# A hybrid decoder layer on one core: row multiplies behind the weights' low halves, rotary steps beside a head's values

## The chip, the cores and the metric

The kernel runs on one core of one Trainium2 chip. The metric is the time of one execution on the device in microseconds (us), taken as the median of several runs. A profiled execution is one more run, of which every instruction is known. The engines of the core are TensorE (PE, with PEld for the loads of its weights), VectorE (DVE), ScalarE (ACT), GpSimd (POOL) and SyncE (SP, which only starts transfers); GpSimd starts transfers too (POOLq).

## The reference, cut to what matters

The kernel computes one layer for 512 prompt tokens and 8 x 8 new tokens, together 576 columns, in float32: a half-step FFN, a mixer and a second half-step FFN, each behind an RMS norm that is modulated by a conditioning vector.

```python
h = modulate(rms_norm(x, n1_g), sh1, sc1)
x = x + 0.5 * g1 * swiglu(h, w1_gate, w1_up, w1_down)
h = modulate(rms_norm(x, nm_g), sh2, sc2)
mix, S_new, v_rows = token_mix(h, pos0, S0, w_in, ...)
...
def token_mix(h, pos0, S0, w_in, ...):
    z = h @ w_in
    u, v, q, k, rv, rg, ga, gb = jnp.split(z, SPLIT_POINTS, axis=-1)
    ...
    qh = rotary(q.reshape(B, L, RET_HEADS, RET_DK), pos)
    kh = rotary(k.reshape(B, L, RET_HEADS, RET_DK), pos) * (RET_DK ** -0.5)
    vh = rv.reshape(B, L, RET_HEADS, RET_DV)
    o_r, S_new = retention(qh, kh, vh, S0)
    o_b = head_rms(o_r).reshape(B, L, RET_V) * jax.nn.silu(rg)
    merged = jax.nn.sigmoid(ga) * (o_a @ w_a) + jax.nn.sigmoid(gb) * (o_b @ w_b)
    return merged @ w_o, S_new, v
```

Here `rms_norm(x)` is `x` times one norm per token (a row of 576 numbers) times a gain per channel, and `modulate` multiplies and adds one number per channel. Of rotary the lower and the upper 64 channels of a head of 128 are turned into each other by tables of sines and cosines. There are eight heads with 128 channels of q and k and 256 of values each.

## The kernel before

Channels lie on partitions and the 576 tokens along the free dimension; a product runs in two halves of 288 columns (half 0 and half 1). The matmuls take float32 split into a high and a low part (hi, lo), and each product is the sum of three: high by high, low by high and high by low. Weights come as float32 into `wraw` by SyncE's transfers. ScalarE casts the high part (L180, L662, `W.hi`), VectorE subtracts it for the low part (L181 in `split_w`, L668 or L672 in `put_lo`). Activations are split in the same way (L188 and L189, L557 and L564).

The program goes through these stages, in us of the profiled span: the first FFN and the end of it, `last_down1` (to 446); the *streams* (446 to 750), projections of the normed `x` for q and k of all heads, the heads' gates and the merge's gates, each stream two column blocks of 128, with the results stored to memory by GpSimd's queue; the eight heads (750 to 1130), each with its values, its scores, its output and some work of other parts beside it; the rest of the merge (to 1270); `w_o` and the second FFN.

**The end of the first FFN.** `last_down1` gives each step a name, and the string `INTO_MIX` (L51ff.) is the written order of them. `D31` is the product of `w1_down` for block 3, half 1, with 18 matmuls of 288 columns; `rs31` its residual add, `sq31` and `ad31` the square and its sum for the next norm, `sp31` the store of `x` to `x1d`. `Wh4` and `Wl4` are the high and low parts of the weights of block 4. `rd0` is the matmul that sums the squares of half 0 over the channels (L437); `q00` to `q20` make the norm of it, `x00` and so on the normed operand, `N11h0` (L557 and L564 for the second) its split, and `h0a0` the first product of the streams. A loop at L1194 loads the weights' blocks in the order 2, 3, 6, 7, 4, 5.

**The streams.** `stream` takes the pairs one by one, each 144 matmuls of 288 columns, and lets generators work beside it by due times in us. One of them is `operands_of_values` (L1239). The heads' values are products of the whole normed `x`, and this generator makes it from memory, block by block: the row of norms (`row`, from `rowd`) is loaded by GpSimd's queue, and so is block `c` of `x` (`x1d`, L1248). Then VectorE multiplies the block by the row (L1254), ScalarE modulates the prompt's columns (L1256), VectorE the new tokens' (L1260, twice), ScalarE casts the high part (L1262) and VectorE makes the low one (L1264). The multiply of block `c` is written behind the load of block `c + 1`, about a stream apart. In a stream ScalarE also does the copy `sn` (L653) of a partial sum, which a matmul needs next, casts of weights (L662) and the sigmoid or silu at the end (L1155).

**The heads.** For each head, `fetch` loads q and k of the head, as stored by the streams. `rotary` (L1315) is six VectorE instructions for the two: L1317 and L1318 multiply halves by the sines into a new block `y`, L1319 multiplies by the cosines, and GpSimd adds the two (L1320). In the code it stands in the work of the head before, at its end. `values_of` makes the head's values (L1342: four products of 24 matmuls), `core` the scores (L1370, which need k and q), and so on. The output parts are split and multiplied beside this. L1505 is the matmul of the new tokens' state update and L1509 the sum of it with the old state on VectorE; these sums free the banks in which the matmuls accumulate, and L478 is the matmul of products that use the bank after.

**What sets the order.** The code is written as one sequence, and a scheduler lets instructions on VectorE, ScalarE and GpSimd change places when one is free before the other. `in_order` adds an order between two instructions without a wait, and `run` keeps the order of the named steps. Buffers come from pools: `slot` hands out a ring of blocks of 576 columns one after another, and a block is free again when its readers are through.

Of the kernel before, what the change touches and what calls it, by code (L numbers as in the profile page):

```python
# [49 lines left out]
"""  # L50
INTO_MIX = """
D00 D01 rs00 Wh2 sp00 sq00 ad00 Wl2 D10 rs01 px0 Wh3 sq01 ad01 Wl3 D11 sp01 rs10 sp10 sq10
ad10 Wh6 D20 rs11 Wl6 px1 sq11 sp11 ad11 D21 Wh7 rs20 sq20 Wl7 sp20 ad20 D30 rs21 Wh4 px2
sq21 Wl4 sp21 ad21 D31 rs30 sq30 sp30 ad30 Wh5 Wl5 D40 rs31 px3 sq31 sp31 nh0 D50 ad31 rs40
sq40 nl0 sp40 ad40 D60 rs50 sq50 wh0 ad50 sp50 wl0 D70 rs60 sq60 sp60 nh1 ad60 D41 rs70 nl1
sq70 sp70 ad70 D51 rs41 wh1 px4 sq41 wl1 sp41 ad41 rd0 rs51 D61 rq0 px5 q00 sq51 q10 sp51
ad51 q20 x00 D71 x10 b000 b010 x20 b100 x30 b110 N11h0 rs71 N11h1 rs61 px7 b210 N11l0 px6
sq71 N11l1 sq61 sp61 sp71 b300 ad61 h0a0 b310 b200 ad71 B21h3 B21h2 B21l3 B21l2 rd1 sn0 h0a1
rq1 q01 q11 q21 x01 h0b0 x11 b01 b00 s0 b11 s1 b10 tx0 sn1 tx1 N1h0 x21 h0b1 N1h1 N1l0 N1l1
b20 x31 b21 T2a1 b31 b30 h1a0 s3 e0s1 s2 B22h3 N3c1 B22h2 T2b1 N3h1 B22l2 p2bh T2h1 B22l3  # L60
# [21 lines left out]
def layer_kernel(ctx: ExitStack, tc: tile.TileContext, a):  # L82
# [95 lines left out]
    def split_w(raw, eng=None):  # L178
        hi, lo = high_low(list(raw.shape[1:]))
        ACT.copy(out=hi, in_=raw)  # L180
        (eng or DVE).tensor_tensor(out=lo, in0=raw, in1=hi.bitcast(F32), op=ALU.subtract)  # L181
        return hi, lo

    def load_w(src, k0, kc, c0, cols, eng=None):
# [471 lines left out]
    class Weights:  # L656
# [8 lines left out]
        def put_lo(self, names):  # L665
            hl, src, neg = self.hl[names]
            if neg:
                DVE.scalar_tensor_tensor(  # L668
                    out=hl[:, 1], in0=src, scalar=-1.0, in1=hl[:, 0].bitcast(F32), op0=ALU.mult, op1=ALU.subtract
                )  # L670
            else:
                DVE.tensor_tensor(out=hl[:, 1], in0=src, in1=hl[:, 0].bitcast(F32), op=ALU.subtract)  # L672
            for i, m in enumerate(names):
                self.w[m] = (hl[:, 0, i], hl[:, 1, i])

# [510 lines left out]
    def last_down1(W, product):  # L1186
        finish(rest)
        gate, g, ps, rest_of = gate1m(), a2(), {}, {}
        warm(AF.Abs_reciprocal_sqrt)
        ops.clear()  # L1190
        ops["near"] = ("B22", "N3", "N4")
        O = Operands(g, 3)
        steps = {}
        for c in (2, 3, 6, 7, 4, 5):  # L1194
            W.load(c)
            steps[f"Wh{c}"] = lambda c=c: W.hi(c)
            steps[f"Wl{c}"] = lambda c=c: W.lo(c)
        w = rg(0), rg(1)
        p = {i: Plain2(w[i][0], i, w[i][1].out, w[i][1].post) for i in range(2)}
        pairs[3] = p[2] = pair2(qk(0))  # L1200
        steps.update(operand_steps(O))
        ends = pair_steps(p, None)
        for n in ("Gh0", "Gl0", "Gh1", "Gl1"):
            ends.pop(n)
        steps.update(ends)
        for c, h in LAST:
            def d(c=c, h=h):
                ps[c, h] = product(c, h)

            def rs(c=c, h=h):  # L1210
                rest_of[c] = resid(xs[c], ps[c, h], c, h, gate)

            steps[f"D{c}{h}"], steps[f"rs{c}{h}"] = d, rs
            steps[f"sq{c}{h}"] = lambda c=c, h=h: n2.square(xs[c], h)
            steps[f"ad{c}{h}"] = lambda h=h: n2.sum(h)
            steps[f"sp{c}{h}"] = lambda c=c, h=h: nc.scalar.dma_start(out=x1d[:, c, HALF[h]], in_=xs[c][:, HALF[h]])
            if h:
                steps[f"px{c}"] = lambda c=c: rest_of[c]()
        for h in range(2):
            norm_steps(steps, n2, O, h)  # L1220

            def q2(h=h):
                n2.q(2, h)
                POOL.dma_start(out=rowd[:, HALF[h]], in_=n2.r[h])

            steps[f"q2{h}"] = q2
        run(INTO_MIX, steps)
# [11 lines left out]
    def operands_of_values():  # L1239

        g = a2()
        row = slot([P, T])
        POOL.dma_start(out=row, in_=rowd)
        come = []
        for c in range(KC + 1):
# [5 lines left out]
                yield 14.0  # L1251
                continue
            c, t = c - 1, come[c - 1]
            DVE.tensor_tensor(out=t, in0=t, in1=row, op=ALU.mult)  # L1254
            yield 2.0
            ACT.activation(  # L1256
                out=t[:, 0:NP], in_=t[:, 0:NP], func=AF.Identity, scale=g[:, c, 0:1], bias=mT[:, 24 + c, 0:1]
# [55 lines left out]
        return t  # L1313

    def rotary(x):  # L1315
        rope, y = tks["rope"], slot([P, T])
        DVE.tensor_tensor(out=y[0:64], in0=x[64:128], in1=rope[64:128, 1], op=ALU.mult)  # L1317
        DVE.tensor_tensor(out=y[64:128], in0=x[0:64], in1=rope[0:64, 1], op=ALU.mult)  # L1318
        DVE.tensor_tensor(out=x, in0=x, in1=rope[:, 0], op=ALU.mult)  # L1319
        POOL.tensor_tensor(out=x, in0=x, in1=y, op=ALU.add)  # L1320
# [9 lines left out]
            S0.append(t)  # L1330
        tks["states"] = hc, S0

    def values_of(hd, wv):
        rv = []
        for n in range(4):
            ps = bank()
# [7 lines left out]
            if n % 2 == 0:  # L1344
                rv.append(slot([P, 2, DV]))
            ACT.copy(out=rv[n // 2][:, n % 2, :], in_=ps[:, :DV])
            tick(24 * 0.109)
        rvs = rts[0].tile([P, DV], F32, tag="rvs", name=nm("rvs"), bufs=2)
        ps = bank()
# [340 lines left out]
    for hd in range(HEADS):  # L1690
        wv = [load_w(win, 4 * i, 4, RV0 + hd * DV, DV) for i in range(2)]
        if hd:
            states(hd)
        rv, rvs = values_of(hd, wv)
        if hd == 0:
            for x in rows[0][:2]:
                rotary(x)
        OBs.append([])
        q, k, *gates = rows.pop(hd)
        prev = core(hd, q, k, gates, rv, rvs, OBs[hd])  # L1700
# [5 lines left out]
        for i, (weights, f) in enumerate(work):  # L1706
# [7 lines left out]
                    fetch_mixers()  # L1714
            if i == len(work) - 2 and i:
                ready = work[i + 1][0]()
                for x in rows[hd + 1][:2]:
                    rotary(x)
        if len(work) == 2:
            for x in rows[hd + 1][:2]:  # L1720
                rotary(x)
        if hd + 1 < HEADS:
            finish(prev)
        if hd == HEADS - 2:
# [323 lines left out]
```

## Time and profile before

| | us |
|---|---|
| median of 3 runs | 1682.55 |
| lowest and highest | 1680.50, 1685.21 |
| the profiled execution | 1680.16 |
| its span in the trace | 1678.3 |
| TensorE busy (98%) | 1641.8 |
| VectorE busy (69%) | 1156.4 |
| ScalarE busy (47%) | 785.2 |
| GpSimd busy (17%) | 291.0 |

The span is the time from the first to the last instruction of the trace, and the profiled execution's own time holds the 1.9 us around it too. The mean granted clock of TensorE is 0.996 of full speed over the span. The busy time is the sum of the durations of an engine's instructions: the instructions of one engine stand in one queue, so an instruction that waits holds back all behind it. A wait is shown in square brackets behind an instruction, as the idle time of the engine before it and what ended that. The rows are in the section before the prediction.

### The profile page before, as it was taken

What the parts mean: (1) busy time and instruction counts of PE and PEld (TensorE: products, weight loads), DVE (VectorE), ACT (ScalarE), POOL (GpSimd) and SP (SyncE); (2) the same over time, 40 slices, a digit from 0 to 9 for tenths busy, and PEclk for the clock granted to TensorE, in tenths of its full rate; (3) what the DMA queues carried; (4) which work ended last, traced back from release to release, by engine and by line L of the source; (5) the groups of instructions that cost most, each with busy time, mean ns of one, the idle gap of its engine ahead of it and who ended that gap; (6) DMA issues with size and microseconds to landing.
All of it is one profiled execution on the core that took longest, in us unless ns stands there. A gap on an engine that the chain in (4) does not pass through costs nothing.

```text
span 1678.3 us, 31363 instructions
## 1 busy us (share of the span) xinstructions
PE 1641.8 (98%) x12548; PEld 1577.9 (94%) x12548; DVE 1156.4 (69%) x1835; ACT 785.2 (47%) x1331; POOL 291.0 (17%) x372
## 2 busy tenths in 40 slices
PE   8999999999999999999999999999999999999997
PEld 4899999999999998899999999998999999999997
DVE  6867847576797776655697654676848868576773
ACT  5633524344564566544444444443236525343453
POOL 0000000000311111013335442444231000000002
PEclk9999999999999999999999999999999999999999
DMA  9553444342547766664457475789640333232331
GB/s 302 146 152 101 141 141 122 113 116 86 166 136 217 218 204 207 192 208 152 141 180 236 157 171 167 210 234 276 185 139 6 93 91 95 86 98 77 100 88 57
DMA packets 300212, 252.09 MB, mean 150 GB/s; under 512 B 13593, under 2 KB 260633, under 8 KB 300066
## 3 DMA queue, kind: packets, MB, share of 16 engines
q1 hardware_dynamic: 284594, 206.76, 40.7%
q0 software_dynamic: 13168, 40.97, 8.8%
q10 hardware_dynamic: 2304, 2.36, 0.4%
q8 instruction: 98, 1.61, 0.4%
q14 instruction: 48, 0.39, 0.1%
HBM read 207.01 MB, written 43.02 MB: 149 GB/s over the span
## 4 chain that ended last, share of the span: by engine, by line
PE 79%; issue 7%; DVE 5%; DMA 3%; ACT 3%; POOL 1%; SPq 1%; POOLq 0%; DVEq 0%; ACTq 0%
PE ps L644 34%; PE ps L478 29%; PE ps L1342 5%; PE ps L1570 2%; PE ps L300 2%; ACT whl L662 1%; PE ps L1470 1%; PE ps L1353 1%; PE ps L1432 1%; DMA wraw<-in_w_down_dram 1%; DVE whl L672 1%; DMA xa<-in_w_ada_dram 1%; DMA c<-x1d 1%; PE ps L1476 1%; PE ps L1448 0%
## 5 line engine op out<-in xcount | busy, mean ns | idle before, releaser
L644 PE MATMUL ps<-xa,whl 128*128 128x288 f32 x3000 | 422.9, 295 | 4.6 <-ACT whl L662 1.4
L644 PEld LDWEIGHTS ps<-xa,whl 128*128 128x128 f32 x3000 | 403.5, 190 | 17.8 <-issue 5.0
L644 PE MATMUL ps<-xs,whl 128*128 128x288 f32 x2040 | 291.2, 296 | 4.8 <-ACT sn L653 4.3
L644 PEld LDWEIGHTS ps<-xs,whl 128*128 128x128 f32 x2040 | 276.2, 190 | 15.5 <-ACT sn L653 8.6
L672 DVE TENSOR_TENSOR whl<-wraw,whl 128x1024 fp32r<-128x1024 f32 x192 | 234.7, 1225 | 56.4 <-ACT whl L662 50.0
L662 ACT CAST whl<-wraw 128x1024 fp32r<-128x1024 f32 x192 | 200.4, 1049 | 103.1 <-DVE wraw L786 62.1
L478 PEld LDWEIGHTS ps<-c,wd 128*128 128x128 f32 x1824 | 242.3, 188 | 3.4 <-issue 3.4
L478 PE MATMUL ps<-c,wd 128*128 128x288 f32 x1824 | 245.4, 295 | 0.0
L478 PE MATMUL ps<-c,whl 128*128 128x288 f32 x1368 | 191.1, 297 | 4.5 <-DVE S L1509 3.4
L478 PEld LDWEIGHTS ps<-c,whl 128*128 128x128 f32 x1368 | 182.8, 188 | 7.2 <-DVE S L1509 4.1
L465 POOL TENSOR_TENSOR x<-x,s 128x64 f32<-128x64 f32 x72 | 36.0, 499 | 811.8 <-DVE s L464 784.6
L459 DVE SCALAR_TENSOR_TENSOR x<-ps,gate,x 128x288 f32<-128x288 f32 (+1 forms) x128 | 61.2, 481 | 116.4 <-PE ps L478 116.3
L181 DVE TENSOR_TENSOR whl<-wraw,whl 128x1024 fp32r<-128x1024 f32 x56 | 79.5, 1422 | 73.3 <-ACT whl L180 72.9
L653 ACT COPY sn<-ps 128x288 f32<-128x288 f32 x195 | 77.2, 398 | 103.1 <-PE ps L644 102.6
L945 ACT CAST wd<-wraw 128x640 fp32r<-128x640 f32 (+2 forms) x58 | 45.4, 783 | 106.3 <-PE ps L478 100.3
L1342 PE MATMUL ps<-whl,xx 128*128 128x256 f32 x768 | 91.6, 280 | 0.0
L1342 PEld LDWEIGHTS ps<-whl,xx 128*128 128x128 f32 x768 | 90.8, 188 | 0.0
L180 ACT CAST whl<-wraw 128x1024 fp32r<-128x1024 f32 x56 | 58.6, 1048 | 28.2 <-PE ps L478 16.1
L662 ACT CAST whs<-wraw 128x512 fp32r<-128x512 f32 x62 | 38.5, 622 | 66.7 <-PE ps L644 58.5
L644 PE MATMUL ps<-xs,whs 128*128 128x288 f32 x480 | 69.7, 293 | 0.0
L644 PEld LDWEIGHTS ps<-xs,whs 128*128 128x128 f32 x480 | 65.5, 189 | 0.0
L950 DVE TENSOR_TENSOR wd<-wraw,wd 128x640 fp32r<-128x640 f32 (+2 forms) x58 | 53.7, 926 | 10.3 <-ACT wd L945 10.3
(285 smaller groups left out, 2228.3 us busy)
## 6 DMA issues: line engine op xcount, KB each, us to landing
ada<-in_w_ada_dram SPq DMA_DIRECT2D x56, 512.0 KB
wraw<-in_w_in_dram SPq DMA_DIRECT2D x96, 256.0 KB
wraw<-in_w_gate_dram SPq DMA_DIRECT2D x88, 256.0 KB
wraw<-in_w_up_dram SPq DMA_DIRECT2D x88, 256.0 KB
wraw<-in_w_in_dram SPq DMA_DIRECT2D x32, 512.0 KB
wraw<-in_w_down_dram SPq DMA_DIRECT2D x32, 384.0 KB
wraw<-in_w_down_dram SPq DMA_DIRECT2D x32, 320.0 KB
accd<-c POOLq DMA_DIRECT2D x32, 288.0 KB, 5.6
```

The costliest lines, as they stand in the source:

```text
L180: ACT.copy(out=hi, in_=raw)
L181: (eng or DVE).tensor_tensor(out=lo, in0=raw, in1=hi.bitcast(F32), op=ALU.subtract)
L459: DVE.scalar_tensor_tensor(out=x[:, o:o + w], in0=ps[:, :w], scalar=g[:, c, 0:1], in1=x[:, o:o + w], op0=ALU.mult, op1=ALU.add)
L465: return lambda: POOL.tensor_tensor(out=x[:, NP:T], in0=x[:, NP:T], in1=u, op=ALU.add)
L478: PE.matmul(ps[:, :H], lhsT=s[:, k, c0:c0 + P], rhs=m[:, HALF[h]], start=k == 0 and z == 0, stop=k == kc - 1 and z == 2,)
L644: PE.matmul(ps[:, :H], lhsT=s[:, j * P:(j + 1) * P], rhs=m[:, j, :], start=fresh and j == 0 and z == 0, stop=j == 3 and z == 2, skip_group ...
L653: ACT.copy(out=t, in_=ps[:, :H])
L662: ACT.copy(out=hl[:, 0], in_=src)
L672: DVE.tensor_tensor(out=hl[:, 1], in0=src, in1=hl[:, 0].bitcast(F32), op=ALU.subtract)
L945: ACT.copy(out=hl[:, 0], in_=self.raw[c])
L950: DVE.tensor_tensor(out=lo, in0=self.raw[c], in1=hi.bitcast(F32), op=ALU.subtract)
L1342: PE.matmul(ps[:, :DV], lhsT=s, rhs=m, start=i == 0, stop=i == 23)
```

## The change

There are four edits.

1. In `INTO_MIX`, `D31` moves from its place ahead of `D40` to behind `D70`, and so `D40`, `D50`, `D60` and `D70` move one product ahead. The weights' blocks are loaded in the order 2, 3, 6, 4, 5, 7. Behind `rd0` there are now three products (`D51`, `D61`, `D71`) until `h0a0`, and not two.
2. `now["lo"]` holds the last low part made of weights (by `split_w` or `put_lo`), and the multiply by the row and the first instruction of a rotary are put behind it by `in_order`.
3. The row of norms gets a tile of its own from the pool of the sums (`tp`, tag "all") and not a block of the ring.
4. The rotary of q and of k moves into `values_of` of its own head: q's behind the second product of values, k's behind the fourth.

```diff
 INTO_MIX = """
...
-ad10 Wh6 D20 rs11 Wl6 px1 sq11 sp11 ad11 D21 Wh7 rs20 sq20 Wl7 sp20 ad20 D30 rs21 Wh4 px2
-sq21 Wl4 sp21 ad21 D31 rs30 sq30 sp30 ad30 Wh5 Wl5 D40 rs31 px3 sq31 sp31 nh0 D50 ad31 rs40
-sq40 nl0 sp40 ad40 D60 rs50 sq50 wh0 ad50 sp50 wl0 D70 rs60 sq60 sp60 nh1 ad60 D41 rs70 nl1
-sq70 sp70 ad70 D51 rs41 wh1 px4 sq41 wl1 sp41 ad41 rd0 rs51 D61 rq0 px5 q00 sq51 q10 sp51
-ad51 q20 x00 D71 x10 b000 b010 x20 b100 x30 b110 N11h0 rs71 N11h1 rs61 px7 b210 N11l0 px6
+ad10 Wh6 D20 rs11 Wl6 px1 sq11 sp11 ad11 D21 Wh4 rs20 sq20 Wl4 sp20 ad20 D30 rs21 Wh5 px2
+sq21 Wl5 sp21 ad21 D40 rs30 sq30 sp30 ad30 Wh7 Wl7 D50 rs40 sq40 sp40 nh0 ad40 D60 rs50
+sq50 nl0 sp50 ad50 wh0 D70 rs60 sq60 sp60 wl0 ad60 D31 rs70 sq70 nh1 sp70 ad70 nl1 D41 rs31
+px3 sq31 sp31 rd0 wh1 D51 ad31 rq0 rs41 px4 q00 sq41 wl1 q10 sp41 ad41 q20 D61 rs51 px5 x00 sq51
+sp51 ad51 D71 x10 b000 b010 x20 b100 x30 b110 N11h0 rs71 N11h1 rs61 px7 b210 N11l0 px6
...
-        (eng or DVE).tensor_tensor(out=lo, in0=raw, in1=hi.bitcast(F32), op=ALU.subtract)
+        now["lo"] = (eng or DVE).tensor_tensor(out=lo, in0=raw, in1=hi.bitcast(F32), op=ALU.subtract)
...
-        for c in (2, 3, 6, 7, 4, 5):
+        for c in (2, 3, 6, 4, 5, 7):
             W.load(c)
...
-        row = slot([P, T])
+        row = tp.tile([P, T], F32, tag="all", name=nm("row"), bufs=1)
...
-            DVE.tensor_tensor(out=t, in0=t, in1=row, op=ALU.mult)
+
+            in_order([now["lo"], DVE.tensor_tensor(out=t, in0=t, in1=row, op=ALU.mult)])
...
-        DVE.tensor_tensor(out=y[0:64], in0=x[64:128], in1=rope[64:128, 1], op=ALU.mult)
+        in_order([
+            now["lo"], DVE.tensor_tensor(out=y[0:64], in0=x[64:128], in1=rope[64:128, 1], op=ALU.mult)
+        ])
...
-    def values_of(hd, wv):
+    def values_of(hd, wv, qk):
...
             ACT.copy(out=rv[n // 2][:, n % 2, :], in_=ps[:, :DV])
+            if n % 2:
+                rotary(qk[n // 2])
             tick(24 * 0.109)
...
-        rv, rvs = values_of(hd, wv)
-        if hd == 0:
-            for x in rows[0][:2]:
-                rotary(x)
+        rv, rvs = values_of(hd, wv, rows[hd][:2])
...
-                for x in rows[hd + 1][:2]:
-                    rotary(x)
-        if len(work) == 2:
-            for x in rows[hd + 1][:2]:
-                rotary(x)
```

`put_lo` (L668 and L672) sets `now["lo"]` in the same way as `split_w`.

VectorE, late in the streams, as a difference. `whl` and `whs` are weights, `c_7524` the block of `x` whose load had just come before, and `c_7228` the block before it; L1254 of before is L1255 of after, and L1260, L1264 are L1261, L1265.

```order
 L672 TENSOR_TENSOR whl_7493<-wraw_7475,whl_7493 128x1024
-L1254 TENSOR_TENSOR c_7524<-c_7524,c_5467 128x576
+L1255 TENSOR_TENSOR c_7228<-c_7228,row_5467 128x576
+L1261 TENSOR_TENSOR c_7228<-c_7228,gain_4543 128x64
+L1261 TENSOR_TENSOR c_7228<-c_7228,mT 128x64
 L890 TENSOR_TENSOR c_7546<-ps_7511,sn_7509 128x288
 L672 TENSOR_TENSOR whs_7629<-wraw_7621,whs_7629 128x512
-L1260 TENSOR_TENSOR c_7524<-c_7524,gain_4543 128x64
-L1260 TENSOR_TENSOR c_7524<-c_7524,mT 128x64
+L1265 TENSOR_TENSOR xx_5404<-c_7228,xx_5404 128x576
 L672 TENSOR_TENSOR whl_7626<-wraw_7620,whl_7626 128x1024
```

At this place the multiply now takes the earlier block; the one of `c_7524` comes a stream later.

VectorE at the state updates of head 2 and the beginning of head 3, before: `c_9876` and `c_9877` are q and k of head 3, `S` the states, and `whl_10376` weights of products.

```order
L189 TENSOR_TENSOR c_10047<-c_9977,c_10046 128x576
L1317 TENSOR_TENSOR c_10092<-c_9876,rope 64x576
L1318 TENSOR_TENSOR c_10092<-c_9876,rope 64x576
L1317 TENSOR_TENSOR c_10097<-c_9877,rope 64x576
L1319 TENSOR_TENSOR c_9876<-c_9876,rope 128x576
L1318 TENSOR_TENSOR c_10097<-c_9877,rope 64x576
L181 TENSOR_TENSOR whl_10376<-wraw_10374,whl_10376 128x1024
L1319 TENSOR_TENSOR c_9877<-c_9877,rope 128x576
L1509 SCALAR_TENSOR_TENSOR S_1276_9602<-S_1276_9602,ps_10131 128x512
```

The same place after; L1515 is L1509 of before, and between the two pieces stand the other updates and the norm of the output.

```order
L189 TENSOR_TENSOR c_10047<-c_9977,c_10046 128x576
L181 TENSOR_TENSOR whl_10376<-wraw_10374,whl_10376 128x1024
L1515 SCALAR_TENSOR_TENSOR S_1274_9592<-S_1274_9592,ps_10121 128x512
...
L189 TENSOR_TENSOR c_10108<-c_9975,c_10107 128x576
L189 TENSOR_TENSOR c_10110<-c_9976,c_10109 128x576
L1320 TENSOR_TENSOR c_10281<-c_9876,rope 64x576
L1322 TENSOR_TENSOR c_10281<-c_9876,rope 64x576
L1323 TENSOR_TENSOR c_9876<-c_9876,rope 128x576
L1320 TENSOR_TENSOR c_10345<-c_9877,rope 64x576
```

The six rotary steps have moved from ahead of the state updates to behind the two splits L189 that stood after them. Heads 4 to 7 have the same pattern, and head 7 has eight mask steps (L1667, now L1673) between the two splits and the rotary.

VectorE at the beginning of head 2, before: `c_9360` and `c_9361` are q and k, and L1601 to L1628 are layer-norm steps of the other half of the mixer.

```order
L1317 TENSOR_TENSOR c_9580<-c_9360,rope 64x576
L1318 TENSOR_TENSOR c_9580<-c_9360,rope 64x576
L1317 TENSOR_TENSOR c_9585<-c_9361,rope 64x576
L1319 TENSOR_TENSOR c_9360<-c_9360,rope 128x576
L1318 TENSOR_TENSOR c_9585<-c_9361,rope 64x576
L1601 BN_AGGR mv<-stats 128x2
L1601 BN_AGGR mv<-stats 64x2
L1319 TENSOR_TENSOR c_9361<-c_9361,rope 128x576
```

The same place after.

```order
L1320 TENSOR_TENSOR c_9653<-c_9360,rope 64x576
L1322 TENSOR_TENSOR c_9653<-c_9360,rope 64x576
L1607 BN_AGGR mv<-stats 128x2
L1607 BN_AGGR mv<-stats 64x2
L1323 TENSOR_TENSOR c_9360<-c_9360,rope 128x576
L1608 TENSOR_SCALAR three<-mv 128x5
L181 TENSOR_TENSOR whl_9886<-wraw_9884,whl_9886 128x1024
L1320 TENSOR_TENSOR c_9711<-c_9361,rope 64x576
L1322 TENSOR_TENSOR c_9711<-c_9361,rope 64x576
L1609 TENSOR_SCALAR three<-three 128x5
L1634 SCALAR_TENSOR_TENSOR c_8671<-c_8671,mv,c_9368 128x512
L1323 TENSOR_TENSOR c_9361<-c_9361,rope 128x576
```

Here k's three steps have moved behind the split L181 and the last of them behind L1634 as well. On TensorE the order of the matmuls is the same but for the place of `D31`, and no engine has an instruction more or less.

## Rows read from the trace of the kernel before

**Rows 1.** The page: the span, and each engine's busy time and instructions.

```profile
span 1678.3 us, 31363 instructions
...
PE 1641.8 (98%) x12548; PEld 1577.9 (94%) x12548; DVE 1156.4 (69%) x1835; ACT 785.2 (47%) x1331; POOL 291.0 (17%) x372
```

**Rows 2.** The waits: engine and line, who ended it: us in total, times, longest.

```profile
PE ps L478 <- DVE S L1509: 3.4, 3, 1.8
PE ps L1370 <- POOL c L1320: 1.7, 1, 1.7
...
DVE c L1254 <- DMA c<-x1d: 8.8, 5, 4.0
```

**Rows 3.** Timeline at 653: start us, us, engine line op out<-in xcount [idle before <-releaser].

```profile
648.82 0.82 ACT L1256 ACTIVATE c<-c,mT,gain 128x512 f32<-128x512 f32 x1 [1.68 <-DVE c L1254]
...
653.46 3.44 PE L644 MATMUL ps<-xs,whl 128*128 128x288 f32 x24 [2.14 <-ACT sn L653]
```

**Rows 4.** Timeline at 680; last, of windows: us, busy PE PEld DVE ACT POOL, PEclk, DMA, GB/s.

```profile
670.49 1.23 DVE L672 TENSOR_TENSOR whl<-wraw,whl 128x1024 fp32r<-128x1024 f32 x1 [0.67 <-ACT whl L662]
...
675.71 0.76 DVE L1254 TENSOR_TENSOR c<-c,c 128x576 f32<-128x576 f32 x1 [4.00 <-DMA c<-x1d]
...
676.51 0.82 ACT L1256 ACTIVATE c<-c,mT,gain 128x512 f32<-128x512 f32 x1 [3.33 <-DVE c L1254]
...
680.29 4.98 PE L644 MATMUL ps<-xs,whl 128*128 128x288 f32 x24 [1.91 <-ACT sn L653]
...
680.00:685.00 5.00, 4.71 (x24) 4.71 (x25) 4.86 (x8) 2.04 (x4) 0.14 (x1) 0.66 0.02 7
```

**Rows 5.** Timeline at the state updates of head 2.

```profile
895.32 1.06 ACT L180 CAST whl<-wraw 128x1024 fp32r<-128x1024 f32 x1
...
896.93 1.11 PE L1505 MATMUL ps<-c,c 128*128 128x256 f32 x8
...
898.47 1.99 POOL L1320 TENSOR_TENSOR c<-c,c 128x576 f32<-128x576 f32 x1 [2.21 <-DVE c L1319]
...
899.20 2.34 DVE L181 TENSOR_TENSOR whl<-wraw,whl 128x1024 fp32r<-128x1024 f32 x1
...
902.26 2.47 DVE L1509 SCALAR_TENSOR_TENSOR S<-S,ps 128x512 f32<-128x512 f32 x4
...
902.99 1.85 PE L478 MATMUL ps<-c,whl 128*128 128x288 f32 x12 [1.79 <-DVE S L1509]
```

**Rows 6.** Timeline ahead of head 2's scores; last, L1320: count: min/median/max ns, first and last start.

```profile
858.92 0.75 DVE L1317 TENSOR_TENSOR c<-c,rope 64x576 f32<-64x576 f32 x1
...
863.03 1.67 DVE L1319 TENSOR_TENSOR c<-c,rope 128x576 f32<-128x576 f32 x1
...
864.84 1.21 DVE L181 TENSOR_TENSOR whl<-wraw,whl 128x1024 fp32r<-128x1024 f32 x1
...
864.86 2.48 POOL L1320 TENSOR_TENSOR c<-c,c 128x576 f32<-128x576 f32 x1
...
865.97 1.39 DVE L1603 TENSOR_SCALAR three<-three 128x5 int32<-128x5 int32 x1
...
867.28 0.74 DVE L1628 SCALAR_TENSOR_TENSOR c<-c,mv,c 128x512 f32<-128x512 f32 x1
...
867.79 1.05 PE L1370 MATMUL ps<-c,c 128*128 128x128 f32 x8
...
L1320 POOL TENSOR_TENSOR c<-c,c x16: 1421/1978/2478, 759.7 to 1103.0; 128x576 f32<-128x576 f32 x16
```

**Rows 7.** Timeline of TensorE at the beginning of the streams.

```profile
447.77 0.40 PE L644 MATMUL ps<-xa,whl 128*128 128x288 f32 x1 [1.29 <-ACT xa L557]
448.64 3.30 PE L644 MATMUL ps<-xa,whl 128*128 128x288 f32 x23 [0.47 <-DVE xa L564]
```

**Rows 8.** Timeline ahead of head 7's scores.

```profile
1111.48 2.69 DVE L1667 TENSOR_TENSOR c<-c,c 64x64 f32<-64x64 f32 x8
...
1119.20 1.05 PE L1370 MATMUL ps<-c,c 128*128 128x128 f32 x8
```

More of the change, by code (lines that the diff above doesn't have):

```diff
@@ L667, in put_lo @@
             if neg:
-                DVE.scalar_tensor_tensor(
+                now["lo"] = DVE.scalar_tensor_tensor(
                     out=hl[:, 1], in0=src, scalar=-1.0, in1=hl[:, 0].bitcast(F32), op0=ALU.mult, op1=ALU.subtract
@@ L671, in put_lo @@
             else:
-                DVE.tensor_tensor(out=hl[:, 1], in0=src, in1=hl[:, 0].bitcast(F32), op=ALU.subtract)
+                now["lo"] = DVE.tensor_tensor(out=hl[:, 1], in0=src, in1=hl[:, 0].bitcast(F32), op=ALU.subtract)
             for i, m in enumerate(names):
```

## The prediction, made before the changed kernel was run

> **What bounds the kernel now.** I first read the page: TensorE's matmuls are busy for 1641.8 of 1678.3 us [rows 1], and no matmul is added or taken away by the change. So only two things can move the time: stretches in which TensorE stands still, and stretches in which its clock is at the lower level. The list of waits comes next, TensorE's part of it [rows 2]: it says who ended each standstill. Two of its lines name work that the change moves: 3.4 us in three waits for the state updates at L1509, and 1.7 us for a rotary sum. A line of VectorE in the same view says that the multiply by the row of norms waited 8.8 us in five places for `x` from memory. Then the timeline of each such place tells what stood ahead of the late instruction, and who waited in the end: in two of the five it was TensorE [rows 3, 4].
>
> **Streams, the stop before 653.46.** TensorE waits 2.14 us for the copy `sn` [rows 3]. ScalarE's modulation L1256 had waited 1.68 us for VectorE's multiply (which waited for the DMA), and what ScalarE does next, that copy in the end, stands behind it. In the new order the multiply stands behind the last low split of a stream (the first order piece above), and the block that it takes was asked for a stream earlier, so its data are there and the 1.68 go; the modulation itself (0.82) moves ahead into time in which ScalarE has nothing to do. Together that is 2.5, more than TensorE's 2.14; I take 2.0 gained, since ScalarE's casts come closer together (bounds 0, if ScalarE's own work is as late, and 2.14).
>
> **Streams, the stop before 680.29.** The same chain [rows 4]: 4.00 us of VectorE waiting for the DMA, 3.33 us of ScalarE waiting for VectorE, `sn` at 679.84, 1.91 us of TensorE. Behind it TensorE's granted clock is 0.66 on average over 5 us, and 24 matmuls take 4.98 us, which took 3.44 after the other stop [rows 3, 4]. So 1.91 + (4.98 - 3.44) = 3.45, taken as 3.4 (bounds 0 and 3.45; if the stop goes and the clock falls all the same, 1.9). The stop at 653.46 was the longer one and its matmuls are at full speed, so I don't count a fall of the clock for each stop.
>
> What stays open in the streams is ScalarE's order. The modulation now stands between the copy `sn` and the cast of the next half weight, of 0.82 us. Where it must wait for VectorE it holds that cast back. Nothing in the trace shows this order. Bounds: no gain is to be had from it; nothing is lost if TensorE has the weights in stock, and 0.82 us in each of eight streams, 6.6, if it never has. In the rows of the stop at 680.29 the split ahead of the multiply is over at 671.7, far ahead of the use, so I take 0.
>
> **Heads 3 to 7, the state updates.** At 902.99 TensorE waits 1.79 us for a bank that L1509 has to empty [rows 5]. Its sums are there when the products of L1505 end, at 898.04, and VectorE only comes at 902.26: ahead of it stood six rotary steps, and a low split that took 2.34 us beside the rotary sum of GpSimd. The new order puts L181 and the updates right behind a split, and the rotary behind the next two (the second pair of order pieces). L181 may start when ScalarE's cast ends, 895.32 + 1.06 = 896.38, and takes some 1.2 [rows 6]; the four updates of 2.47 end near 900.2. TensorE wants the bank at 902.99 - 1.79 = 901.2. So all of the 1.79 goes, and with the same order the two other waits of this line: 3.4 in all (bounds 2.4, if the second and third keep 0.5 each, and 3.4). Behind it, VectorE is no later: the rotary fills the space in which it waited for the weights of values.
>
> **Head 2, a loss.** Here k's rotary now stands behind a low split and a layer-norm step (the third pair). Before, VectorE went from 858.92 to 867.28 through six rotary steps, the split and some small ones; 0.91 of that is the k multiply of 1.67 that waited for GpSimd, and up to 1.39 is a small step beside the second sum [rows 6]. In the new order the k multiply ends after the same steps and one L1628 of 0.74: 867.28 - 0.91 + 0.74 = 867.1, without the small step's wait 865.7. The sum on GpSimd is 1.42 at least, 1.98 in the middle, 2.48 at most: 867.1 to 869.6. The scores begin at 867.79, and TensorE did not wait for them. So the loss is 0 to 1.8. Taken is the middle of the two starts, 866.4, the middle price 1.98, and half of q's sum (0.7) for its meeting VectorE on the way: 869.1, that is 1.4 lost (with all of q's sum, 2.4, the upper bound).
>
> That meeting is the place where a rule speaks against the change. In the trace the split L181 takes 1.21 when it starts ahead of GpSimd's sum and 2.34 when the sum started first; then the split ends 1.1 us after the sum does [rows 5, 6]. The Trainium skill, "SBUF — State Buffer", section "SBUF: two separate sides", says why: VectorE with two inputs from SBUF and a GpSimd operation that reads SBUF take the shared ports in turn, for a whole instruction each. By that rule head 2 loses 1.4 and the sum is as below; were the two free of each other, nothing would be lost there and the sum were 1.4 better. The trace agrees with the rule.
>
> **Head 7 and head 0.** In head 7 eight mask steps of 2.69 stand ahead of the new rotary place. They began at 1111.48 [rows 8]; VectorE comes up to 4.2 earlier to the updates ahead of them, as in [rows 5], less what it then waits for ScalarE's cast, for which I take 0.9: they end near 1110.9. Six rotary steps of 0.76 end at 1115.5, up to 1.4 later with GpSimd in between, and the sum of 1.42 to 1.98 ends at 1117 to 1118.9. The scores, at 1119.20 before, are wanted 0.8 earlier, at 1118.4: loss 0 to 0.5, taken 0.2. Head 0 waited 1.70 for its sum [rows 2]; its rotary keeps its steps and changes places with one split of 1.2 and its sum with the stores on GpSimd's queue: -0.5 to +0.5, taken 0.
>
> **Into the streams, at 447.** The half-0 products of the norm now have three products of `w1_down` behind them instead of two, so the first wait, 1.29 for ScalarE's operand, has 18 more matmuls as cover (some 2.6 us at the 3.30/23 of a matmul there) and goes [rows 7]. But TensorE needs L564's result one matmul later, and VectorE makes that only behind the two residual adds of the last products, as before; TensorE goes on at 448.64 when it is there. The end is earlier by 0.3 at most in that order, and all 1.29 + 0.47 = 1.76 go if VectorE's part comes early. Taken -0.3 (bounds 0 and -1.76).
>
> The row of norms loaded into its own tile, and the load's new place on GpSimd's queue ahead of five stores, cost nothing: the first multiply is now a stream later than that load. If the cover were gone, it would be one landing, 4.00 as in [rows 4].
>
> **The sum.** -2.0 - 3.4 - 3.4 - 0.3 + 1.4 + 0.2 = -7.5. The profiled execution of before took 1680.16 us, so its like would take 1672.7. It is 2.4 below the median of the runs shown, 1682.55; the forecast is of a median: 1682.55 - 7.5 = 1675.0. About 0.3%, 5 us, is what a measurement of this kernel can tell from no change: faster is below 1677.5, slower above 1687.6.
>
> **Rivals.** *ScalarE's order eats the streams' gain.* The modulation waits behind VectorE and holds the weights' cast: up to 6.6 back, of which the streams have 5.4 to give: 1680.4, and with half of it 1677.7. For it: the order is untried and ScalarE carries both. Against: VectorE now has the data, so the wait is one multiply of 0.76 at most. *Only a part does what it says.* If the waits in the streams are someone else's, ScalarE's own work for one, the heads alone give -2.1: 1680.5; if the heads lose at heads 2, 7 and 0 at their bounds (2.4 + 0.5 + 0.5) and the lower clock follows the new stop (1.5), they give +1.5: 1678.3 with the streams. *Slower: k's sum late in every head.* The rotary begins only when the products of the head's values run; if VectorE and GpSimd hinder each other on all six steps, the scores of each of the eight heads wait for the sum, as head 0 does today for 1.70. With the slowest sum as price, 2.48, that is 8 x 2.48 = 19.8 against a gain of 9.1: +10.7, 1693. It decides from (9.1 + 5.0)/8 = 1.8 a head. Against it: heads 3 to 7 gain 3 us and more of VectorE's time ahead of that place [rows 5], and head 7, with the masks ahead, is the tightest and still near zero. *More than forecast.* The whole 1.76 at 447 and nothing lost in heads 2 and 7: 1672.0.
>
> **How the numbers follow.** Forecast (1672.5 to 1677.5) 0.50; more than it 0.08; ScalarE's order or a part only (1677.5 to 1683) 0.35; slower 0.07. Faster is 0.58, same 0.35, slower 0.07. The range from 1670.5 to 1682.5 leaves out the slower case and the rims of the others.
>
> **What would show it.** In the trace after: no wait of VectorE for `x1d`; no stop of TensorE for `sn` near 651 and 676 and the clock at full speed there; no wait of L478 for the state updates; and a stop of 1 to 2 us ahead of head 2's scores, with GpSimd's sum as its releaser. A new line of TensorE waiting for a half weight in the streams would prove the first rival, waits for the rotary sum in several heads the slower one. I am wrong if the stops vanish and the time does not follow, or if a new stop in the streams takes their place.

## The result, and the profile after

| | before | after |
|---|---|---|
| median of runs in the same session | 1681.49 us (6 runs) | 1672.99 us (6 runs) |
| ratio, 95% interval | | 0.9949 [0.9939, 0.9959] |
| the profiled execution's span | 1678.3 us | 1670.8 us |

The changed kernel is 8.5 us faster between the medians, 0.51% by the ratio (8.6 us), and the interval goes from 0.41% to 0.61% (6.9 to 10.3 us), so it is faster by more than the 5 us that a measurement can tell. A second session gave 0.9950 [0.9934, 0.9966] (below).

TensorE's waits after, in the same view as [rows 2] (who waited for whom: us in total, times, longest), behind the span and the busy times of the page:

```profile
span 1670.8 us, 31364 instructions
...
PE 1639.0 (98%) x12548; PEld 1576.0 (94%) x12548; DVE 1153.5 (69%) x1835; ACT 783.8 (47%) x1331; POOL 288.1 (17%) x372
```

```profile
PE ps L1376 <- POOL c L1324: 1.9, 2, 1.0
PE ps L1414 <- POOL h L1409: 1.8, 1, 1.8
...
PE ps L644 <- ACT xa L557: 0.9, 1, 0.9
PE ps L644 <- DVE xa L564: 0.7, 1, 0.7
...
PE ps L644 <- ACT sn L653: 0.6, 3, 0.2
```

The 3.4 us for the state updates are gone from this list, and of the waits for `sn` only three small ones outside the streams are left. Against that, the rotary sum (L1324, L1320 of before) now stops TensorE in two heads instead of one, and there is a wait that did not exist: for GpSimd's copy L1409 (L1403 of before). At 447 one wait has shrunk from 1.29 to 0.9 and the other grown from 0.47 to 0.7 [rows 7].

Here is the place that answers to [rows 3], and last the one of [rows 4], from the timelines of VectorE, ScalarE and TensorE (start us, us, engine line op out<-in xcount [idle before <-releaser]):

```profile
645.09 1.23 DVE L672 TENSOR_TENSOR whl<-wraw,whl 128x1024 fp32r<-128x1024 f32 x1 [0.67 <-ACT whl L662]
...
646.23 0.75 DVE L1255 TENSOR_TENSOR c<-c,row 128x576 f32<-128x576 f32 x1
...
647.02 0.82 ACT L1257 ACTIVATE c<-c,mT,gain 128x512 f32<-128x512 f32 x1 [1.03 <-DVE c L1255]
...
647.74 0.60 ACT L662 CAST whs<-wraw 128x512 fp32r<-128x512 f32 x1
...
652.17 3.43 PE L644 MATMUL ps<-xs,whl 128*128 128x288 f32 x24
...
676.75 3.32 PE L644 MATMUL ps<-xs,whl 128*128 128x288 f32 x24
```

The multiply follows the split at once and waits for no transfer. ScalarE still waits for it (1.03), the cast behind that comes late by little, and TensorE goes on without a stop at both places, at full clock: 24 matmuls in 3.3 to 3.4 us, with a granted clock of 1.00 from 652 to 657 and from 676 to 681.

The state updates of head 2, which answer to [rows 5]:

```profile
894.51 1.23 DVE L181 TENSOR_TENSOR whl<-wraw,whl 128x1024 fp32r<-128x1024 f32 x1 [2.14 <-ACT whl L180]
895.65 2.47 DVE L1515 SCALAR_TENSOR_TENSOR S<-S,ps 128x512 f32<-128x512 f32 x4
...
895.98 4.93 PE L478 MATMUL ps<-c,whl 128*128 128x288 f32 x36
```

The updates start as soon as their products are there, and TensorE's 36 matmuls run in one piece where they were cut into 24 and 12.

To see what each place is worth, I followed the starts of the same matmuls in the two traces. A negative number says that the trace after is ahead, and the last column what was gained or lost since the line above.

| place | before | after | difference | since the last |
|---|---|---|---|---|
| first FFN | 202.41 | 203.86 | +1.45 | |
| second matmul of the streams | 448.64 | 450.00 | +1.36 | -0.1 |
| before the stop at 653 | 647.92 | 648.85 | +0.93 | -0.4 |
| behind it | 656.74 | 655.44 | -1.30 | -2.2 |
| before the stop at 680 | 674.97 | 673.49 | -1.48 | -0.2 |
| behind it | 685.46 | 680.25 | -5.21 | -3.7 |
| first values of head 0 | 746.56 | 742.16 | -4.40 | +0.8 |
| scores of head 0 | 766.22 | 761.11 | -5.11 | -0.7 |
| last values of head 2 | 864.30 | 859.18 | -5.12 | 0.0 |
| head 2's matmuls on k's copies | 869.52 | 867.58 | -1.94 | +3.2 |
| values of head 3 | 904.68 | 900.75 | -3.93 | -2.0 |
| values of head 5 | 1004.96 | 999.97 | -4.99 | -1.1 |
| values of head 7 | 1105.25 | 1099.18 | -6.07 | -1.1 |
| scores of head 7 | 1119.20 | 1113.12 | -6.08 | 0.0 |

The places of the change add up to -0.1 - 2.2 - 3.7 - 0.7 + 3.2 - 4.2 = -7.7. What lies between them is not the change: +1.45 before the streams, -0.4 and -0.2 in them, and +0.8 at 704, where eight small matmuls on weights of the conditioning take 2.10 us instead of 1.30. Behind the heads the trace of before has another stretch at the lower clock, at 1314 (20 matmuls in 4.45 us), which the trace after does not have (2.88), though the stops ahead of it are the same in both (1.37 and 0.83, 1.37 and 0.82). So of the 7.5 us between the two spans 6.1 lie ahead of head 7's scores, and most of the rest is this difference in the clock. The table explains these two executions; the 8.5 us between the medians agree with it within their interval.

### The profile page after: what moved, and what is told of

Read it like the earlier page. It is cut to its first block, busy times and chain, and to the rows that moved or that the text cites. A ratio compares the mean times of both kernels' runs of the same rounds, so it can differ in the third digit from the quotient of the medians.

```text
span 1670.8 us, 31364 instructions
## 1 busy us (share of the span) xinstructions
PE 1639.0 (98%) x12548; PEld 1576.0 (94%) x12548; DVE 1153.5 (69%) x1835; ACT 783.8 (47%) x1331; POOL 288.1 (17%) x372
## 5 line engine op out<-in xcount | busy, mean ns | idle before, releaser
L672 DVE TENSOR_TENSOR whl<-wraw,whl 128x1024 fp32r<-128x1024 f32 x192 | 234.8, 1225 | 56.5 <-ACT whl L662 45.8
L459 DVE SCALAR_TENSOR_TENSOR x<-ps,gate,x 128x288 f32<-128x288 f32 (+1 forms) x128 | 61.1, 481 | 117.2 <-PE ps L478 117.1
L181 DVE TENSOR_TENSOR whl<-wraw,whl 128x1024 fp32r<-128x1024 f32 x56 | 75.6, 1351 | 71.2 <-ACT whl L180 70.8
```

The costliest lines, as they stand in the source:

```text
L181: now["lo"] = (eng or DVE).tensor_tensor(out=lo, in0=raw, in1=hi.bitcast(F32), op=ALU.subtract)
L459: DVE.scalar_tensor_tensor(out=x[:, o:o + w], in0=ps[:, :w], scalar=g[:, c, 0:1], in1=x[:, o:o + w], op0=ALU.mult, op1=ALU.add)
L672: now["lo"] = DVE.tensor_tensor(out=hl[:, 1], in0=src, in1=hl[:, 0].bitcast(F32), op=ALU.subtract)
```

## The experiments

Each was timed beside the kernel before, and the ratio is to that kernel unless it says otherwise. A difference of 0.001 is 1.7 us.

**The streams' part alone.** The kernel before with the edits of the multiply (`put_lo` sets `now["lo"]` too) and the row's tile:

```diff
-        (eng or DVE).tensor_tensor(out=lo, in0=raw, in1=hi.bitcast(F32), op=ALU.subtract)
+        now["lo"] = (eng or DVE).tensor_tensor(out=lo, in0=raw, in1=hi.bitcast(F32), op=ALU.subtract)
...
-        row = slot([P, T])
+        row = tp.tile([P, T], F32, tag="all", name=nm("row"), bufs=1)
-            DVE.tensor_tensor(out=t, in0=t, in1=row, op=ALU.mult)
+            in_order([now["lo"], DVE.tensor_tensor(out=t, in0=t, in1=row, op=ALU.mult)])
```

> The kernel before with the second edit for the row multiply and the third edit alone (multiply behind the last low part, the row in its own tile); INTO_MIX and the rotary as before. Theory (the two stops for sn go, and the lower clock behind the second with them): 2.14 + 1.91 + 1.5 = 5.5 us faster than before, no wait of VectorE for x1d. Rival (the fall of the clock at 680 is chance and no part of the change): 4.0 faster. Rival (the stops only go because the new INTO_MIX shifts the streams): 0 to 1 faster, both stops still there.

Measured: 0.9968 [0.9956, 0.9979], 5.4 us faster. No stop for `sn` is left in the streams, and the multiply waits for `x1d` nowhere. (The list of waits names `x1d` once, 2.10 us ahead of the sum L890 at 610.9, here and in the trace after; in the trace of before the same sum waits 2.07, with TensorE as the releaser, and no multiply and no stop of TensorE hangs on it.) The rival that the new order of `INTO_MIX` did it is out: that order is not in this kernel. The 5.5 of the theory and the 4.0 of the other rival both lie within the interval, from 3.5 to 7.4.

**The rotary's part alone**, in `values_of` and without the old calls, `now["lo"]` kept.

```diff
-        DVE.tensor_tensor(out=y[0:64], in0=x[64:128], in1=rope[64:128, 1], op=ALU.mult)
+        in_order([
+            now["lo"], DVE.tensor_tensor(out=y[0:64], in0=x[64:128], in1=rope[64:128, 1], op=ALU.mult)
+        ])
...
+            if n % 2:
+                rotary(qk[n // 2])
...
```

> The kernel before with the fourth edit and the rotary's part of the second alone (rotary in its own head's values, behind the last low part); streams and INTO_MIX as before. Theory: the three waits for the state updates go (-3.4), head 0's wait shrinks by 0.7, head 2 loses the 2.76 that the profile after shows (0.94 before its scores, 1.82 before the matmuls on GpSimd's copies): 1.3 us faster than before, at the edge of what can be told. Rival (head 2's two waits come from the streams' part, by another phase of the buffers): 4.1 faster, no stop in head 2. The stop at 680 is still there, and its clock shows whether the fall comes each time.

Measured: 0.9987 [0.9978, 0.9995], 2.2 us faster (0.8 to 3.7). The three waits for the updates are gone, and head 2 has the same two new stops, 0.94 and 1.82. So these come from the rotary's part, and not from another phase of the buffers; the 4.1 of the rival lie outside the interval. Which of its two edits moves the updates ahead, the new place or the order behind the low part, was not tried apart. The other question, the clock, was answered otherwise than I had thought: both stops for `sn` are there, and neither has the lower clock behind it (granted 1.00 over the 5 us from 654.4 and from 680.4):

```profile
654.40 3.42 PE L644 MATMUL ps<-xs,whl 128*128 128x288 f32 x24 [2.60 <-ACT sn L653]
...
680.46 3.44 PE L644 MATMUL ps<-xs,whl 128*128 128x288 f32 x24 [1.15 <-ACT sn L653]
```

**`INTO_MIX` alone**, the string as in the change.

```diff
-        for c in (2, 3, 6, 7, 4, 5):
+        for c in (2, 3, 6, 4, 5, 7):
...
```

> The kernel before with the first edit alone (INTO_MIX and the order of the weights' loads). Theory: the wait for ScalarE's operand shrinks and VectorE's takes its place, 0 to 0.3 us faster, that is the same. Rival (the whole transition comes earlier): 1.8 faster. Both stops for sn are still there by the theory, and their clocks are a third look at the fall at 680.

Measured: 1.0004 [0.9995, 1.0012], the same. The wait for ScalarE's operand fell from 1.29 to 0.94 and VectorE's rose from 0.47 to 0.66. Here both stops for `sn` have the lower clock behind them (granted 0.66 over the 5 us from 654.5, 0.68 from 683.5):

```profile
654.60 4.97 PE L644 MATMUL ps<-xs,whl 128*128 128x288 f32 x24 [2.85 <-ACT sn L653]
...
683.52 4.84 PE L644 MATMUL ps<-xs,whl 128*128 128x288 f32 x24 [2.47 <-ACT sn L653]
```

The three parts together give 0.9968 x 0.9987 x 1.0004 = 0.9959, and all of the change 0.9949; the gap is within the intervals, so no working together of the parts is needed to explain the result.

**The multiply without its order.** The changed kernel, but for this:

```diff
-            in_order([now["lo"], DVE.tensor_tensor(out=t, in0=t, in1=row, op=ALU.mult)])
+            DVE.tensor_tensor(out=t, in0=t, in1=row, op=ALU.mult)
```

> The changed kernel without the order between the last low part and the row multiply (the rest as changed, the row's own tile too). Theory (the order is what takes the multiply away from its DMA): both stops for sn are back, VectorE waits for x1d, 4 us slower than the changed kernel, and up to 3 more if the clock falls at both stops. Rival (the row's own tile or the new INTO_MIX took the stops away): within 1 us of the changed kernel.

Measured: 0.9980 [0.9970, 0.9990], that is 5.2 us slower than the changed kernel; the intervals of the two do not meet. VectorE waits for `x1d` again, 8.5 us in five places, and both stops are back, the first with the lower clock behind it (granted 0.66 over the 5 us from 653.5) and the second without (1.00 from 681.5):

```profile
653.66 4.95 PE L644 MATMUL ps<-xs,whl 128*128 128x288 f32 x24 [2.25 <-ACT sn L653]
...
681.68 3.42 PE L644 MATMUL ps<-xs,whl 128*128 128x288 f32 x24 [1.60 <-ACT sn L653]
```

**The row in the ring again.**

```diff
-        row = tp.tile([P, T], F32, tag="all", name=nm("row"), bufs=1)
+        row = slot([P, T])
```

> The changed kernel with the row of norms in a block of the ring again (third edit undone). Theory (the tile of its own costs and gives nothing; the multiply's order does it): within 0.5 us of the changed kernel, no stop for sn. Rival (the ring's phase or the earlier load of the row matters): the waits for x1d come back in part, 1 to 5 us slower than the changed kernel.

Measured: 0.9947 [0.9934, 0.9960], as the changed kernel. No stop for `sn`, the stops in head 2 are the same 0.93 and 1.82. So the tile of its own gives and costs nothing that can be told, and the order alone takes the two stops away.

**The blocks of `x` asked for earlier, with the order of before.**

```diff
-            if c < KC:
-                come.append(slot([P, T]))
-                POOL.dma_start(out=come[c], in_=x1d[:, c])
+            for _ in range(2 if c == 0 else 1):
+                if len(come) < KC:
+                    come.append(slot([P, T]))
+                    POOL.dma_start(out=come[-1], in_=x1d[:, len(come) - 1])
```

> The kernel before, only with the blocks of x asked for one block (about a stream) earlier; no order between weights and multiply, the row in the ring, INTO_MIX and rotary as before. Theory (the two stops are the landing of x, whatever keeps the multiply off it): VectorE waits for x1d nowhere late, both stops for sn go or shrink under 0.5, 4 to 5.5 us faster than before. Rival (the multiply and the modulation are late by their place among the weights' casts and table loads, and only the new order mends that): the stops stay over 1 us each, within 2 us of before.

Measured: 0.9982 [0.9971, 0.9993], 3.0 us faster: between the two. The stop at 680 is gone, the one at 653 has grown to 3.01 us (at full clock behind it), and VectorE still waits for the transfer there:

```profile
643.83 0.54 POOL L1249 DMA_DIRECT2D c<-x1d  x1
...
649.72 0.76 DVE L1255 TENSOR_TENSOR c<-c,c 128x576 f32<-128x576 f32 x1 [3.51 <-DMA c<-x1d]
...
655.16 3.42 PE L644 MATMUL ps<-xs,whl 128*128 128x288 f32 x24 [3.01 <-ACT sn L653]
```

The multiply that waits is that of the block issued at 643.83, though the code asks for it a stream ahead. Where nothing holds the multiply back the scheduler moves it ahead by as much as the load: each of the multiplies from 513 to 650 starts 3.8 to 5.9 us behind the issue of the latest load, as in the kernel before (3.8 to 6.1), and the landings of this kernel take 3.7 to 5.8. Two blocks are loaded at the start, so no load stands near 669 any more, and that is why the stop at 680 is gone. So the wait is the landing, as the theory says; but the remedy was not the earlier request, as I expected of this run, it is the order.

**Head 2's rotary at its old place.** The changed kernel, but for head 2 (the calls for it stand at the end of head 1's work):

```diff
-            if n % 2:
+            if n % 2 and hd != 2:
                 rotary(qk[n // 2])
...
+        if hd == 1:
+            for x in rows[2][:2]:
+                rotary(x)
         if hd + 1 < HEADS:
             finish(prev)
```

> The changed kernel with the rotary of head 2 alone at its old place in the code (the end of head 1's work); all other heads as changed. Theory (k's late rotary is what costs head 2 its 2.76): both new stops in head 2 go and it is 2.8 us faster than the changed kernel, 11.3 faster than before. Rival (the stops in head 2 come from the layer-norm steps and the copies on GpSimd meeting VectorE whatever the rotary's place): 0 to 1 faster than the changed kernel.

Measured: 0.9932 [0.9920, 0.9945], and 2.9 us faster than the changed kernel with its 0.9949. Neither stop of head 2 is there, and k's sum comes in time:

```profile
859.94 2.48 POOL L1324 TENSOR_TENSOR c<-c,c 128x576 f32<-128x576 f32 x1
862.48 0.77 POOL L1406 COPY h<-c 128x128 f32<-128x128 f32 x1
...
862.86 1.05 PE L1376 MATMUL ps<-c,c 128*128 128x128 f32 x8
```

The two numbers come from different sessions, so I ran both once more beside each other.

> The changed kernel once more, beside the next. As before it: 8 to 9 us faster than the kernel before, the two new stops in head 2 of 0.94 and 1.82.

> The changed kernel with head 2's rotary alone at its old place, once more, on the same chip as the changed kernel. Theory: 2.8 us faster than it, no stop in head 2. Rival: under 1 us.

Measured: the changed kernel 0.9950 [0.9934, 0.9966], with head 2 at the old place 0.9937 [0.9921, 0.9953]. The stops of the changed kernel were there again (0.93 and 1.82), those of the other not. By the ratios the version is ahead of the changed kernel both times, by 2.9 and 2.2 us, but the intervals overlap, and beside each other the medians are only 1.1 us apart (1671.64 and 1670.51). So the traces show that the two stops go with the late rotary of k; that the time follows is likely, and its size open. Against the kernel before the version is faster by 11.4 and 10.6 us.

**Head 2's copies on ScalarE.** Why does the stop of 1.82 come? In the trace after:

```profile
860.93 0.75 DVE L1323 TENSOR_TENSOR c<-c,rope 128x576 f32<-128x576 f32 x1
...
861.76 1.95 POOL L1324 TENSOR_TENSOR c<-c,c 128x576 f32<-128x576 f32 x1 [2.22 <-DVE three L1612]
...
863.66 0.73 DVE L1634 SCALAR_TENSOR_TENSOR c<-c,mv,c 64x512 f32<-64x512 f32 x1
863.76 1.16 PE L1376 MATMUL ps<-c,c 128*128 128x128 f32 x8 [0.94 <-POOL c L1324]
863.77 3.52 POOL L1406 COPY h<-c 128x128 f32<-128x128 f32 x1
...
864.39 1.21 DVE L181 TENSOR_TENSOR whl<-wraw,whl 128x1024 fp32r<-128x1024 f32 x1
...
865.93 1.21 DVE L181 TENSOR_TENSOR whl<-wraw,whl 128x1024 fp32r<-128x1024 f32 x1
...
867.24 0.29 POOL L1409 COPY h<-c 128x128 f32<-128x128 f32 x1
...
867.58 0.44 PE L1414 MATMUL ps<-ident,h 128*128 128x128 f32 x2 [1.82 <-POOL h L1409]
```

k's multiply ends at 861.68, the sum at 863.71, and the scores, wanted at 862.82, wait 0.94. The copy L1406, which takes 0.29 us in most heads, then takes 3.52, beside one layer-norm step, two splits and some shorter steps of VectorE, and the matmuls that need both copies wait. The experiment moves the copies:

```diff
+        copy = ACT.copy if hd == 2 else POOL.tensor_copy
-        POOL.tensor_copy(
+        copy(
...
-        POOL.tensor_copy(
+        copy(
...
```

> The changed kernel with the two copies of k's last 64 columns (L1406, L1409) of head 2 on ScalarE instead of GpSimd. Theory (the 1.82 us ahead of the matmuls on the copies come from GpSimd's first copy, 3.52 us where it took 0.77 before, since VectorE's two-input steps hold it): the stop of 1.82 goes, the 0.94 ahead of the scores stays, 1.8 us faster than the changed kernel. Rival (the copies are only late because k's sum is late): the stop shrinks by less than a microsecond, or comes again at the next use.

Measured: 0.9940 [0.9928, 0.9952], 1.5 us faster than the changed kernel by the medians, with overlapping intervals. In the trace the theory holds: 0.92 stays, 1.82 is gone and doesn't come again. What now follows the sum on GpSimd is stretched instead, 4.14 us for a product that takes 1.29 at the median of the eight heads, and nobody waits for that:

```profile
863.50 4.14 POOL L1388 TENSOR_TENSOR c<-c,hc 128x512 f32<-128x512 f32 x1
...
863.57 0.30 ACT L1407 COPY h<-c 128x128 f32<-128x128 f32 x1 [1.58 <-POOL c L1324]
...
865.43 0.38 PE L1415 MATMUL ps<-ident,h 128*128 128x128 f32 x2
```

**k's sum of head 2 on VectorE.**

```diff
-    def rotary(x):
+    def rotary(x, eng=None):
...
-        POOL.tensor_tensor(out=x, in0=x, in1=y, op=ALU.add)
+        (eng or POOL).tensor_tensor(out=x, in0=x, in1=y, op=ALU.add)
...
-                rotary(qk[n // 2])
+                rotary(qk[n // 2], DVE if hd == 2 and n == 3 else None)
```

> The changed kernel with the sum of k's rotary of head 2 on VectorE instead of GpSimd; the place of the rotary unchanged. Theory (GpSimd's sum, 1.95 us at the end of the chain, costs the 0.94): VectorE's sum takes 0.75 behind one more layer-norm step, so the scores wait 0 to 0.4, and the copies start earlier on GpSimd but still meet VectorE: 0.6 to 2.5 us faster than the changed kernel. Rival (VectorE's own order is late): the stop ahead of the scores stays near 0.9.

Measured: 0.9941 [0.9928, 0.9953], 1.3 us faster than the changed kernel, again with overlapping intervals. The scores wait 0.43, and the copy takes 1.30, soon enough:

```profile
862.30 1.30 POOL L1406 COPY h<-c 128x128 f32<-128x128 f32 x1 [3.60 <-DVE c L1324]
...
862.38 1.13 PE L1376 MATMUL ps<-c,c 128*128 128x128 f32 x8 [0.43 <-DVE three L1618]
```

(The releaser's name is that of VectorE's next step; the scores need the sum ahead of it.) So both stops hang on GpSimd: without its sum of 1.95 the first falls from 0.94 to 0.43, and the second goes when the copies leave it or when they start earlier, whether by this sum or by the old place of the rotary (0.77 for the copy there).

## Why the prediction was right, and where it was not

The forecast was -7.5 us and 1675.0; measured were -8.5 and 1672.99. Of the 2.0 us between the two times 1.1 lie in the median of before, which was 1681.49 beside the change and 1682.55 in the forecast. The forecast case came, near its faster rim. That the places in the traces add up to -7.7, so close to -7.5, is in part luck: head 2 lost 1.8 us more than put, and the other terms gained 2.0 more. The terms below are measured in the table of places.

*The stop at 653*: -2.0 was put, -2.2 measured, by the mechanism named. The kernels without the order and with the earlier loads show that it is the landing and that the order mends it; those with `INTO_MIX` alone and with the row in the ring, that the other edits don't.

*The stop at 680*: -3.4 was put, -3.7 measured. The stop was right. The lower clock was put wrongly, as part of this stop and of no other. The runs show that it comes behind either of the two, both or neither: it came in 2 of the 5 traces that have the first stop (`INTO_MIX` alone and the multiply without its order; not before, the rotary alone or the earlier loads) and in 2 of the 4 that have the second (before and `INTO_MIX` alone; not the rotary alone or the multiply without its order). Estimated from these few traces, (2/5 + 2/4) x 1.5, that is some 1.4 us for the two on the mean over executions, near the 1.5 that I had put on one, but by chance. For the difference of two single profiles such a term should stand as a range from 0 to 3.

*ScalarE's order in the streams*: taken at nothing, and so it was. ScalarE does wait for the multiply (1.03), as the first rival says, and the cast is late by some 0.3 us, but TensorE has the weights in stock.

*The state updates*: -3.4 was put, -4.2 measured (2.0, 1.1 and 1.1). The three waits went as forecast. The step summed waits as the profile lists them, and a stop costs some 0.25 us more than its wait (1.79 listed and 2.04 lost, 0.80 and 1.06). Part of it lies in how the profile lists ends: the 36 matmuls after have 4.93 us, yet the next ones start 4.77 behind their start, so a run's listed end stands 0.16 behind the place where the next can start. The rest stays open; at head 2 the two stops, 2.76 by their waits, cost 3.2 in the same way.

*Head 2*: +1.4 was put, +3.2 measured, more than the upper bound of 2.4. (The prediction's own times give 1.3, 869.1 against 867.79, and with all of q's sum, 0.7 more, 2.0; the 1.4 and the 2.4 don't follow from them.) The place and the mechanism are right. The scores' part, 0.94, is within the step's 0 to 1.8, though just under the stop of 1 to 2 us that was named as its sign. What the step left out is the next user of k: two small copies stand behind the sum on GpSimd's queue, and the matmuls on them come 1.7 us behind the scores where nothing stops them (862.86 and 864.59 with head 2 at its old place). I costed the sum's meeting with VectorE, and took GpSimd's next instruction, of 0.77 us in the trace of before, as free. It was 3.52.

*Head 7*: +0.2 was put, 0 measured. The masks took 2.69 us before because GpSimd's work met them; behind the move they take 1.16, and k's sum ends at 1111.45, 1.7 us ahead of the scores:

```profile
1102.95 1.16 DVE L1673 TENSOR_TENSOR c<-c,c 64x64 f32<-64x64 f32 x8
...
1110.01 1.44 POOL L1324 TENSOR_TENSOR c<-c,c 128x576 f32<-128x576 f32 x1 [0.69 <-DVE c L1323]
...
1113.12 1.05 PE L1376 MATMUL ps<-c,c 128*128 128x128 f32 x8
```

*Head 0*: 0 was put, -0.7 measured. Its bounds reached to -0.5; k's sum takes 1.40 us there, where it took 2.31.

*The transition at 447*: -0.3 was put, -0.1 measured, and alone the edit changes nothing that can be told. As the step said, the second wait takes the first one's place. The first shrank by a quarter, from 1.29 to 0.95, and did not go: the third product behind the norm's matmul gives it 0.34 us of the 2.6 I had counted. The step left out what VectorE does in between. In the trace after, a split of weights (L672, 1.22 us) stands between the norm's steps at 442.10 and a residual add (L459 and L464, 0.44 and 0.21) at 444.23, where the trace of before has neither, and the four products L526 with the norm take 3.57 us instead of 2.77. So ScalarE's operand starts 8.0 us behind the norm's matmul and not 6.0.

*The slower rival* (k's sum late in every head) needed 1.8 us a head; it came in head 2 alone, with 3.2, and head 0 got better.

## What to carry to other kernels

Here the consumer that the scheduler could place freely ran just behind its load, whether the code asked for the load one stream ahead or two; an order against work that is known to be late enough took it off the landing. When a step is moved, follow its result through the queue of the engine that makes it to the next user and the one after that, with their longest times and not the usual ones: the larger part of the loss came from the second. And count a stop for a little more than its wait, with the lower clock as a chance and not as part of it.

## What the hardware showed that was not expected

Two things. GpSimd's wait for VectorE can last over several of VectorE's instructions: the copy of 0.29 us took 3.52 while a layer-norm step of 0.73 and two splits of 1.21 passed, and the product of 1.29 took 4.14 with such steps beside it. My prediction counted one instruction at a time for each engine, in turns. Why VectorE's next step goes first stays open. The Trainium skill, "SBUF — State Buffer", section "SBUF: two separate sides", says that the two engines hold their shared ports for a whole instruction each. The traces agree with that: the copy ends at 867.29, 0.15 us behind the second split, which kept its usual 1.21. They show in addition that the one that waits need not be the next. That the ports are the reason is the page's account; no run tried it apart.

The granted clock goes to its lower level behind a stop of 1 to 3 us in some executions and not behind a stop of about the same length in others: behind 2.25 us the kernel without the order has it (0.66 over 5 us), behind 2.60 the kernel with the rotary alone does not (1.00), nor does the one with the earlier loads behind 3.01. At the beginning of the streams, where two short waits stand together, 23 matmuls take 3.3 us in most traces and 4.85 in some, as in this line of the kernel with the streams' part alone (granted 0.66 from 448 to 453), for waits of 1.28 and 0.46, as in the trace of the kernel before (3.30 us there, [rows 7], and 1.00 from 447 to 452):

```profile
448.37 4.85 PE L644 MATMUL ps<-xa,whl 128*128 128x288 f32 x23 [0.46 <-DVE xa L564]
```
